# A two-block model on one core: the hybrid layer's elementwise work leaves GpSimd, and block 1's token-major projections run 512 columns per matmul

## The chip, the core and the metric

The kernel runs on one core of a Trainium2 chip. The time is the device time of one execution in microseconds (us); three executions of the kernel before were timed. The engines are written as in the profile: PE (TensorE matmuls), PEld (its weight loads), DVE (VectorE), ACT (ScalarE), POOL (GpSimd) and SP (SyncE, which issues the weight transfers).

## The reference

256 tokens of width 1024 pass through two models one after the other. Block 1 has two layers, each with one large input projection, three branches (differential attention, a gated spatial unit, dilated-window attention) and gated output projections. Block 2 puts 16 meta tokens in front (272 tokens) and has two layers, each of the form feed-forward, mixer, feed-forward. The first mixer is the hybrid one: a forgetting attention ("fox", 8 heads of 64) beside a gated delta rule (4 heads of 128). The second mixer is RWKV-7. Cut to what the change touches:

```python
def layer(x, ...):                                  # block 1, twice
    proj = rmsnorm(x, norm_g) @ w_in                # aq ak av az buv bz cq ck cv cz gates
    ...                                             # attention a, spatial unit b, attention c
    return x + merged @ w_out

def hybrid_attention_mixer(h, w_in, ...):           # block 2, layer 0
    fq, fk, fv, ff, gqkv, ga, gb, gz = split(h @ w_in)
    q, k, v = silu(causal_conv4(gqkv))              # 4 heads of 128
    q, k = l2_normalize(q) / sqrt(128), l2_normalize(k)
    # gated delta rule with decay g and beta, chunked; forgetting attention beside it
    return concat(o_fox, o_gdn) @ w_out
```

## The kernel before

All weights stream from HBM in units of 128x1024 f32 (512 KB). `Stream.unit` (L202 to L213) turns the raw tile `wraw` into a rounded half `wh` by ACT (L210) and the remainder `wl = wraw - wh` (L212), by DVE or, where the stream's rule says so, by POOL. Activations are split in the same way (`xh`, `xl`), and every product is three matmuls: high by high, high by low, low by high. Up to three `wh` and three `wl` tiles exist at a time.

**Block 1.** `proj_tok` (L387) makes the token-major projections: two PSUM banks, one for each 128 tokens, 512 output columns each. Seven such projections are in a layer (cq, ck, cv, aq, ak, av, bv), four units each. A unit holds 4 of the 8 k-tiles for 256 of the 512 columns, so that each matmul writes 256 columns. A `yield` after every three matmuls hands over to `Weave`, which inserts attention steps and delayed pieces (`put_off(n, fn)` runs `fn` after n such steps). The matmuls of these parts carry L96, the line of the helper `Pinned` that fixes their program order; other engines' instructions may be moved by the scheduler.

**The hybrid mixer** (`hybrid`, L985) has 29 units of 24 matmuls. The part called the first stretch below runs units 0 to 12 and then 15, 14, 13: unit 0 gives the small columns, then each head has a k, a q and a v unit. The convolution of each unit is four passes (`cvy`: ACT L1153, then three of DVE, L1155) and a tanh gate (ACT L1157, DVE L1158). Twenty steps later PE turns the result (`ct`), and for q and k `normed` (L1173) takes sums of squares on ACT (L1178), a small power on POOL (`rr`), a halving of it on DVE (L1182) and the scaled copy `kn` on DVE (L1184); twelve steps later PE turns `kn` back (`sm`). `decays` (L1117) makes the decay matrices `iX`, `Ua` and `at`; `gram` (L1203) makes `kqT`, `qd`, and, in `products`, `kd` and `kbe`, all on POOL before. PE runs its instructions in the written order, so that it waits at `sm` for `kn` whatever lies behind. The second stretch begins with `compact16` (L905): the triangular inverse and the delta rule's chunks (`chain`) are interleaved with the fox attention and the units that are left.

Of the kernel before, what the change touches and what calls it, by code (L numbers as in the profile page):

```python
# [371 lines left out]
def block1_layer(c, l, xT, head, pos, ws, w_br, w_out, sgu_w, sgu_b, sgu_gb):  # L372

    nc, tc, ap, tp = c.nc, c.tc, c.b1a, c.b1t
    lam_init = 0.8 - 0.6 * math.exp(-0.3 * l)
    xh, xl, acc = head
# [3 lines left out]
    pe = Pinned(c, nc.tensor)  # L380
    wv = Weave()

    def next_unit():
        unit[0] += 1
        return ws.unit(unit[0] - 1)

    def proj_tok(evac):  # L387

        pss = [bank(c), bank(c)]
        for p in range(2):  # L390
            for kh in range(2):
                wh, wl = next_unit()
                wh4 = wh.rearrange("p (m k c) -> p m k c", m=2, k=4)
                wl4 = wl.rearrange("p (m k c) -> p m k c", m=2, k=4)
                for i in range(2):
                    o = pss[i][:, 256 * p:256 * p + 256].rearrange("p (m c) -> p m c", m=2)
                    for k4 in range(4):
                        k = 4 * kh + k4
                        a, b = xh[:, k, P * i:P * i + P], xl[:, k, P * i:P * i + P]
                        h, w = wh4[:, :, k4, :], wl4[:, :, k4, :]  # L400
                        pe.matmul(o, a, h, start=k == 0, stop=False)
                        pe.matmul(o, a, w, start=False, stop=False)
                        pe.matmul(o, b, h, start=False, stop=k == 7)
                        if p and kh and k4 == 3:
                            evac(i, pss[i])
                        yield

    def rope_T(res, scale):

# [96 lines left out]
    qT, kT, v = qk(), qk(), v2()  # L506
# [135 lines left out]
    vb = [T(c, ap, [P, 512], F32, "vb", bufs=2) for i in range(2)]  # L642
# [27 lines left out]
    pe = nc.tensor  # L670
# [76 lines left out]
    for m in range(KT):  # L747
        wh, wl = wo.unit(m)
# [38 lines left out]
CH = 96  # L787
# [196 lines left out]
def hybrid(c, h, acc, w_in, w_out):  # L984
    nc, tc = c.nc, c.tc  # L985
# [7 lines left out]
    pe, gp = Pinned(c, nc.tensor), Pinned(c, nc.gpsimd)  # L993
    wv = Weave()

    xh, xl = x_pair(c)
    for k in range(KT):
        split(c, xh[:, k, :], xl[:, k, :], h[:, k, :], col(c, "mix0", k))
    ws = Stream(c, w_in, lambda u: u > 3 and (u % 3 == 2 if u < 13 else u % 2 == 0))

    def proj(u, evac):
        wh, wl = ws.unit(u)
# [13 lines left out]
    tri = T(c, cp, [CH, PADT], F32, "tri")  # L1016
# [17 lines left out]
    be, be2 = T(c, ap, [CH, 3, 4], F32, "beta"), T(c, ap, [CH, 3, 4], F32, "beta2")  # L1034
# [5 lines left out]
    gct = T(c, ap, [CH, 3, 4], F32, "gct")  # L1040
    kdf = T(c, ap, [CH, 3, 4], F32, "kdf")
    bgf = T(c, ap, [CH, 3, 4], F32, "bgf")
    U = T(c, ap, [CH, 12, CH], F32, "Ua")
    at = T(c, ap, [CH, 12, CH], F32, "at")
    egc, brc = [t.rearrange("p h (i t) -> p h i t", i=3) for t in (grow, brow)]
# [71 lines left out]
    def decays():  # L1117

        de = T(c, ap, [CH, 12, CH], F32, "iX")
        gp.tensor_sub(de.rearrange("p (h i) t -> p h i t", h=4), egc[:CH],  # L1120
                      gct.rearrange("p i h -> p h i").unsqueeze(3).to_broadcast([CH, 4, 3, CH]))
        nc.vector.tensor_scalar(de, de, 0.0, None, ALU.min)
        keep(nc.scalar.activation(de, de, AF.Exp))

        def masked():
            nc.vector.tensor_mul(U, de, mneg.unsqueeze(1).to_broadcast([CH, 12, CH]))
            gp.tensor_mul(at, de, tri[:, :CH].unsqueeze(1).to_broadcast([CH, 12, CH]))

        wv.put_off(8, masked)
        keep(nc.scalar.activation(egc, egc, AF.Exp))  # L1130
        keep(nc.scalar.activation(kdf, kdf, AF.Exp))
        keep(nc.scalar.activation(bgf, gct, AF.Exp))
        nc.vector.tensor_mul(bgf, bgf, be)


    kd = T(c, ap, [CH, 4, 3, P], F32, "kd")
# [34 lines left out]
    def normed(hd, w):  # L1171


        def then(pt):
            ss = T(c, tp, [CH, 3], F32, "ss", bufs=2)
            for i in range(3):
                sq = T(c, tp, [CH, P], F32, "sqh", bufs=2)
                nc.scalar.activation(sq, pt[:, i, :], AF.Square, accum_out=ss[:, i:i + 1])  # L1178
            nc.vector.tensor_scalar(ss, ss, 0.25, EPS, ALU.mult, ALU.add)
            rr = T(c, tp, [CH, 3], F32, "rr", bufs=2)  # L1180
            gp.tensor_tensor(rr, ss, c.mhalf[:CH, :3], ALU.pow)
            nc.vector.tensor_scalar(rr, rr, 0.5 * P ** -0.5 if w else 0.5, None, ALU.mult)  # L1182
            kn = T(c, tp, [CH, 3, P], F32, f"kn{w}", bufs=2 - w)
            nc.vector.tensor_mul(kn, pt, rr.unsqueeze(2).to_broadcast([CH, 3, P]))  # L1184

            def back():
                pb = bank(c, "sm")
                for i in range(3):
                    pe.transpose(pb[:, CH * i:CH * i + CH], kn[:, i, :], c.ident[:CH, :CH])
                pb3 = pb[:, :PADT].rearrange("p (i t) -> p i t", i=3)  # L1190
                if w == 0:
                    kT = T(c, ap, [P, 3, CH], F32, "kT", bufs=2)
                    nc.scalar.activation(kT, pb3, AF.Copy)
                    KQ[hd] = kT, T(c, ap, [P, 3, 2, CH], F32, "kqT", bufs=2), kn
                else:
                    nc.scalar.activation(KQ[hd][1][:, :, 1, :], pb3, AF.Copy)
                    wv.put_off(12, lambda: gram(hd))

            wv.put_off(12, back)

        return then

    def gram(hd):  # L1203

        kT, kq, kn = KQ[hd]
        gp.tensor_mul(kq[:, :, 0, :], kT, brc[:, hd])
        gp.tensor_mul(qd[:, hd], kq[:, :, 1, :], egc[:, hd])

        def products():
            gp.tensor_mul(kd[:, hd], kn, kdf[:, :, hd:hd + 1].to_broadcast([CH, 3, P]))  # L1210
            gp.tensor_mul(kbe[:, hd], kn, bgf[:, :, hd:hd + 1].to_broadcast([CH, 3, P]))
            for i0, m in ((0, 2), (2, 1)):
                ps = bank(c, "sm")
                for i in range(m):
                    pe.matmul(ps[:CH, 2 * CH * i:2 * CH * (i + 1)], kT[:, i0 + i, :],
                              kq[:, i0 + i].rearrange("p a t -> p (a t)"), start=True, stop=True)
                p4 = ps[:CH, :2 * CH * m].rearrange("p (i a t) -> p i a t", a=2, t=CH)
                for w, o in ((0, U), (1, at)):
                    o = o[:, 3 * hd + i0:3 * hd + i0 + m, :]
                    nc.vector.tensor_mul(o, p4[:, :, w, :], o)  # L1220

        wv.put_off(12 if hd == 0 else 8, products)

    def beta_v(hd):
        def then(pt):
            nc.vector.tensor_mul(vb[:, hd], pt, be2[:, :, hd:hd + 1].to_broadcast([CH, 3, P]))

        return then

# [187 lines left out]
    for hd in range(4):  # L1417
        a = gts[hd]
# [396 lines left out]
def b1_host(I):  # L1815
    a = {}
    a["xT"] = np.ascontiguousarray(I["x"][0].T.reshape(KT, P, TOK1).transpose(1, 0, 2))
    a["pos"] = np.ascontiguousarray(I["positions"].reshape(2, P).T)
    names = ["aq", "ak", "av", "az", "bu", "bv", "bz", "cq", "ck", "cv", "cz", "gA", "gB", "gC"]
    base, n = {}, 0  # L1820
    for nm in names:
        base[nm] = n
        n += 8 if nm[0] == "g" else 4
    order = []
    for nm in ["cq", "ck", "cv", "aq", "ak", "av", "bz", "bu", "bv", "cz", "gC", "gB", "az", "gA"]:
        if nm[1] in "qkv":
            for p in range(2):
                for kh in range(2):
                    order += [(4 * kh + k4, base[nm] + 2 * p + m) for m in range(2) for k4 in range(4)]
        else:  # L1830
            for m in range(8 if nm[0] == "g" else 4):
                order += [(k, base[nm] + m) for k in range(8)]
    br = [(4 * n + k, m) for n in (2, 1, 0) for m in range(8) for k in range(4)]
    sq = [(k, m) for m in range(8) for k in range(8)]
    for l in range(2):

        w = I["w_in"][l]
        qk = w[:, :2 * 512].reshape(D, 2, 2, 2, 2, 64).transpose(0, 1, 2, 4, 3, 5).reshape(D, 1024)
# [125 lines left out]
```

## Time and profile before

| | |
|---|---|
| median of 3 runs | 2030.96 us (2029.15 to 2035.1) |
| the profiled execution's own time | 2033.22 us |
| its span in the profile | 2031.5 us |
| PE, DVE, ACT, POOL busy in the span | 95%, 68%, 48%, 14% |
| the hybrid's first stretch | 838.95 to 923.89 us of the span |
| the hybrid's second stretch | 923.89 to 1039.40 us |

The stretches are read from the trace: the first begins with DVE's first scaled copy of a hybrid projection (L1057), the second with `compact16` and ends where the mixer's output projection begins. Busy shares are means over parts with different limits; what a part is worth is read from that part.

### The profile page before, as it was taken

How to read it: one execution, taken by the hardware profiler on the slowest of the kernel's cores; microseconds unless marked ns; L12 is line 12 of the kernel's file. 1: busy time of each engine (PE TensorE's matmuls, PEld its weight loads, DVE VectorE, ACT ScalarE, POOL GpSimd, SP SyncE). 2: the span in 40 equal slices, each digit the busy share in tenths (PEclk: the TensorE clock that was granted, in tenths of full speed). 3: DMA queues.
4: the chain of work that ended last, by engine and by line, in shares of the span. 5: the costliest groups of instructions: out<-in, count | busy, mean ns of one | idle time of the engine just before them, and what ended most of it. 6: DMA issues, size and time to landing. Idle time of an engine off the chain costs nothing.

```text
span 2031.5 us, 37801 instructions
## 1 busy us (share of the span) xinstructions
PE 1929.5 (95%) x15003; PEld 1858.0 (91%) x15003; DVE 1390.8 (68%) x2896; ACT 973.2 (48%) x1745; POOL 285.1 (14%) x320
## 2 busy tenths in 40 slices
PE   8999999999999999968999999999989879989998
PEld 7889999889999999966999999999988768979998
DVE  6577576577578665787477665666589699846764
ACT  5455355455355444442354444444366535555443
POOL 1113011113010000143010000000044313110000
PEclk9999899999899999987999999999989789989999
DMA  6445466445455555532235555555534100026663
GB/s 200 137 123 160 142 180 181 142 117 161 141 177 176 177 175 174 164 107 63 63 112 169 175 175 176 171 175 174 171 94 135 42 12 1 32 72 180 186 186 115
DMA packets 79461, 280.02 MB, mean 138 GB/s; under 512 B 9890, under 2 KB 12082, under 8 KB 79156
## 3 DMA queue, kind: packets, MB, share of 16 engines
q1 hardware_dynamic: 77088, 275.57, 45.5%
q8 instruction: 118, 1.93, 0.4%
q10 hardware_dynamic: 2196, 2.03, 0.3%
q14 instruction: 59, 0.48, 0.1%
HBM read 276.50 MB, written 1.07 MB: 137 GB/s over the span
## 4 chain that ended last, share of the span: by engine, by line
PE 64%; DVE 9%; ACT 2%; POOL 2%; issue 1%; DVEq 0%; ACTq 0%; POOLq 0%
PE mm L220 17%; PE mm L218 16%; PE mm L219 16%; PE mm L96 4%; PE iv L96 1%; PE iv L946 1%; DVE wl L212 1%; PE fs L96 1%; PE sm L1677 1%; DVE mixt L1523 1%; DVE iYc L925 1%; DVE ish L924 1%; DVE ish L923 0%; PE sm L264 0%; ACT wh L210 0%
## 5 line engine op out<-in xcount | busy, mean ns | idle before, releaser
L210 ACT ACTIVATE wh<-wraw 128x1024 fp32r<-128x1024 f32 x517 | 546.9, 1059 | 603.6 <-PE mm L219 288.8
L212 DVE TENSOR_TENSOR wl<-wraw,wh 128x1024 fp32r<-128x1024 f32 x474 | 587.1, 1239 | 254.9 <-ACT wh L210 249.6
L218 PE MATMUL mm<-xh,wh 128*128 128x272 f32 (+1 forms) x2112 | 607.4, 288 | 5.9 <-ACT xh L1524 3.0
L220 PE MATMUL mm<-xh,wl 128*128 128x272 f32 (+1 forms) x2112 | 606.2, 287 | 6.6 <-DVE wl L212 2.9
L219 PE MATMUL mm<-xl,wh 128*128 128x272 f32 (+1 forms) x2112 | 606.9, 287 | 0.9 <-POOL xl L1526 0.9
L220 PEld LDWEIGHTS mm<-xh,wl 128*128 128x128 f32 x2112 | 401.5, 190 | 9.0 <-DVE wl L212 5.1
L218 PEld LDWEIGHTS mm<-xh,wh 128*128 128x128 f32 x2112 | 399.7, 189 | 7.9 <-ACT xh L1524 3.5
L219 PEld LDWEIGHTS mm<-xl,wh 128*128 128x128 f32 x2112 | 401.1, 190 | 1.9 <-POOL xl L1526 1.3
L218 PE MATMUL mm<-uh,wh 128*128 128x272 f32 (+1 forms) x704 | 201.7, 286 | 0.0
L219 PE MATMUL mm<-ul,wh 128*128 128x272 f32 (+1 forms) x704 | 201.5, 286 | 0.0
L220 PE MATMUL mm<-uh,wl 128*128 128x272 f32 (+1 forms) x704 | 201.0, 286 | 0.0
L212 POOL TENSOR_TENSOR wl<-wraw,wh 128x1024 fp32r<-128x1024 f32 x43 | 103.0, 2396 | 412.4 <-ACT wh L210 368.8
L96 PE MATMUL mm<-wh,xh 128*128 128x256 f32 x448 | 133.9, 299 | 9.2 <-ACT wh L210 9.2
L220 PEld LDWEIGHTS mm<-uh,wl 128*128 128x128 f32 x704 | 133.2, 189 | 0.0
L218 PEld LDWEIGHTS mm<-uh,wh 128*128 128x128 f32 x704 | 132.3, 188 | 0.0
L219 PEld LDWEIGHTS mm<-ul,wh 128*128 128x128 f32 x704 | 132.3, 188 | 0.0
L96 PE MATMUL mm<-wl,xh 128*128 128x256 f32 x448 | 127.4, 284 | 0.7 <-DVE wl L212 0.7
L96 PE MATMUL mm<-wh,xl 128*128 128x256 f32 x448 | 126.6, 283 | 0.0
L96 PE MATMUL mm<-xh,wh 128*128 128x272 f32 (+1 forms) x360 | 120.0, 333 | 0.0
L96 PE MATMUL mm<-xh,wl 128*128 128x272 f32 (+1 forms) x360 | 107.0, 297 | 0.0
L96 PE MATMUL mm<-xl,wh 128*128 128x272 f32 (+1 forms) x360 | 106.8, 297 | 0.0
L96 PEld LDWEIGHTS mm<-wh,xh 128*128 128x128 f32 x448 | 86.1, 192 | 9.2 <-ACT wh L210 9.2
(597 smaller groups left out, 3576.9 us busy)
## 6 DMA issues: line engine op xcount, KB each, us to landing
wraw<-in_ffn_in SPq DMA_DIRECT2D x176, 512.0 KB, 3.6
wraw<-in_w_in SPq DMA_DIRECT2D x136, 512.0 KB, 3.7
wraw<-in_ffn_out SPq DMA_DIRECT2D x88, 512.0 KB, 3.7
wraw<-in_hyb_in SPq DMA_DIRECT2D x29, 512.0 KB, 3.7
wraw<-in_w_br SPq DMA_DIRECT2D x24, 512.0 KB, 3.8
wraw<-in_rw_rkv SPq DMA_DIRECT2D x24, 512.0 KB, 3.8
wraw<-in_w_out SPq DMA_DIRECT2D x16, 512.0 KB, 4.4
wraw<-in_hyb_out SPq DMA_DIRECT2D x8, 512.0 KB, 3.7
```

The source lines that it names most:

```text
L96: return lambda *a, **k: self.tc.keep_in_program_order(f(*a, **k))
L210: nc.scalar.activation(wh, r, AF.Copy)
L212: eng.tensor_sub(wl, r, wh.bitcast(F32))
L218: pe.matmul(ps, lh, rh, start=start, stop=False)
L219: pe.matmul(ps, lh, rl, start=False, stop=False)
L220: pe.matmul(ps, ll, rh, start=False, stop=stop)
L924: nc.vector.tensor_mul(sh, sh, Uc[:, :, j:j + 1].to_broadcast([n, ni, 16 - j]))
L925: nc.vector.tensor_add(Yc[:, :, j:], Yc[:, :, j:], sh)
L946: pe.matmul(ps[:n, n * i:n * i + n], lhs[:, i0 + i, :], rhs[:, i0 + i, :], start=True, stop=True)
L1523: nc.vector.scalar_tensor_tensor(t, xx[:, k, :], col(c, "mu", 8 * i + k), hn[:, k, 1:], ALU.mult, ALU.add)
L1677: nc.tensor.matmul(ps[:, P * q:P * q + P], pair_ht(bd[:, c0 + q]), pair_ht(AR[:, c0 + q]), start=True, stop=True)
```

## The change

In block 1 a unit of a token-major projection now holds 2 of the 8 k-tiles for all 512 columns, and each matmul writes 512 columns; the host packs the weights to match. The number of units, of yields and of columns is as before; the number of matmuls in `proj_tok` halves, from 1344 to 672 over both layers. A step between two yields is now two matmuls and one in turn.

In the hybrid mixer 11 `wl` tiles move from POOL to DVE, as do the decay difference `iX`, the mask of `at`, and the products `kqT` and `qd` (8). `kd` and `kbe` (8 products of 96x384 on POOL) become 24 ACT copies of 96x128 with a factor per token. `kn` (8) and `vb` (4), DVE multiplies before, become 36 ACT copies of the same kind. The halving of `rr` is folded into the constants ahead of the power. POOL keeps the powers and the fills.

```diff
     def proj_tok(evac):
-        for p in range(2):
-            for kh in range(2):
-                wh, wl = next_unit()
...
-                        pe.matmul(o, a, h, start=k == 0, stop=False)
-                        pe.matmul(o, a, w, start=False, stop=False)
-                        pe.matmul(o, b, h, start=False, stop=k == 7)
...
+        for kq in range(4):
+            wh, wl = next_unit()
+            for i in range(2):
+                for k2 in range(2):
...
+                    pe.matmul(pss[i], a, h, start=k == 0, stop=False)
+                    pe.matmul(pss[i], a, w, start=False, stop=False)
+                    yield
+                    pe.matmul(pss[i], b, h, start=False, stop=k == 7)
...
-    ws = Stream(c, w_in, lambda u: u > 3 and (u % 3 == 2 if u < 13 else u % 2 == 0))
+    ws = Stream(c, w_in)
...
-        gp.tensor_sub(de.rearrange("p (h i) t -> p h i t", h=4), egc[:CH],
+        nc.vector.tensor_sub(de.rearrange("p (h i) t -> p h i t", h=4), egc[:CH],
...
-            gp.tensor_mul(at, de, tri[:, :CH].unsqueeze(1).to_broadcast([CH, 12, CH]))
+            nc.vector.tensor_mul(at, de, tri[:, :CH].unsqueeze(1).to_broadcast([CH, 12, CH]))
...
-            nc.vector.tensor_scalar(rr, rr, 0.5 * P ** -0.5 if w else 0.5, None, ALU.mult)
-            nc.vector.tensor_mul(kn, pt, rr.unsqueeze(2).to_broadcast([CH, 3, P]))
+            for i in range(3):
+                nc.scalar.activation(kn[:, i, :], pt[:, i, :], AF.Copy, scale=rr[:, i:i + 1])
...
-        gp.tensor_mul(kq[:, :, 0, :], kT, brc[:, hd])
-        gp.tensor_mul(qd[:, hd], kq[:, :, 1, :], egc[:, hd])
+        nc.vector.tensor_mul(kq[:, :, 0, :], kT, brc[:, hd])
+        nc.vector.tensor_mul(qd[:, hd], kq[:, :, 1, :], egc[:, hd])
...
-            gp.tensor_mul(kd[:, hd], kn, kdf[:, :, hd:hd + 1].to_broadcast([CH, 3, P]))
-            gp.tensor_mul(kbe[:, hd], kn, bgf[:, :, hd:hd + 1].to_broadcast([CH, 3, P]))
+            for i in range(3):
+                nc.scalar.activation(kd[:, hd, i, :], kn[:, i, :], AF.Copy, scale=kdf[:, i, hd:hd + 1])
+                nc.scalar.activation(kbe[:, hd, i, :], kn[:, i, :], AF.Copy, scale=bgf[:, i, hd:hd + 1])
...
-            nc.vector.tensor_mul(vb[:, hd], pt, be2[:, :, hd:hd + 1].to_broadcast([CH, 3, P]))
+            for i in range(3):
+                nc.scalar.activation(vb[:, hd, i, :], pt[:, i, :], AF.Copy, scale=be2[:, i, hd:hd + 1])
```

The scheduler's order on two engines is shown at the place where head 1's k is normed, early in the first stretch. On DVE before, from the clamp of `iX` to the scaled copy `kn` that PE waits for:

```order
L1122 TENSOR_SCALAR iX_10468<-iX_10468 96x1152
L1155 SCALAR_TENSOR_TENSOR cvy_10446<-cvx_10443,cols_80,cvy_10446 128x272
L1179 TENSOR_SCALAR ss_10483<-ss_10483 96x3
L1148 TENSOR_TENSOR cvx_10511<-mm_10461,R_10019 128x272
L1155 SCALAR_TENSOR_TENSOR cvy_10446<-cvx_10443,cols_80,cvy_10446 128x272
L1182 TENSOR_SCALAR rr_10491<-rr_10491 96x3
L212 TENSOR_TENSOR wl_10661<-wraw_10658,wh_10660 128x1024
L1158 SCALAR_TENSOR_TENSOR cvy_10446<-gth_10452,cvy_10446 128x272
L1184 TENSOR_TENSOR kn_1839_10494<-ct_10479,rr_10491 96x384
```

On DVE now, at the same place (lines are three lower; `iX` is no longer made on POOL):

```order
L1117 TENSOR_TENSOR iX_9800<-hgrow_9355,gct_9357 96x1152
L212 TENSOR_TENSOR wl_9859<-wraw_9856,wh_9858 128x1024
L1152 SCALAR_TENSOR_TENSOR cvy_9716<-cvx_9713,cols_80,cvy_9716 128x272
L1119 TENSOR_SCALAR iX_9800<-iX_9800 96x1152
...
L1130 TENSOR_TENSOR bgf_9359<-bgf_9359,beta_9349 96x12
L1123 TENSOR_TENSOR Ua_9360<-iX_9800,mneg_9339 96x1152
L1152 SCALAR_TENSOR_TENSOR cvy_9778<-cvx_9775,cols_80,cvy_9778 128x272
L1178 TENSOR_SCALAR ss_9815<-ss_9815 96x3
L1124 TENSOR_TENSOR at_9361<-iX_9800,tri_9336 96x1152
```

`iX`, `at` and a `wl` have joined DVE's row, `kn` and the halving have left it, and the sums `ss` now stand behind `Ua`.

On ACT before, the same place: the sums of squares of head 1's k, and behind them at once the `wh` of unit 10.

```order
L1178 ACTIVATE sqh_10484,ss_10483<-ct_10479 96x128
L1178 ACTIVATE sqh_10486,ss_10483<-ct_10479 96x128
L1178 ACTIVATE sqh_10488,ss_10483<-ct_10479 96x128
L210 ACTIVATE wh_10660<-wraw_10658 128x1024
L1123 ACTIVATE iX_10468<-iX_10468 96x1152
```

On ACT now, the `wh` of unit 10 is the last row here; the sums of squares of head 1's k stand some twenty instructions ahead of it.

```order
L1183 ACTIVATE kn_1839_9825<-ct_9811,rr_9823 96x128 x3
L1211 ACTIVATE kbe_9363<-kn_1793_9618,bgf_9359 96x128
L1192 ACTIVATE kT_9910<-sm_9906 128x288
L1210 ACTIVATE kd_9362<-kn_1793_9618,kdf_9358 96x128
L1211 ACTIVATE kbe_9363<-kn_1793_9618,bgf_9359 96x128
L1183 ACTIVATE kn_1853_9888<-ct_9874,rr_9886 96x128 x3
L1210 ACTIVATE kd_9362<-kn_1793_9618,kdf_9358 96x128
L1150 ACTIVATE cvy_9919<-cvx_9916,cols_80 128x272
L1154 ACTIVATE gth_9853<-cvy_9847 128x272
L1227 ACTIVATE vb_9364<-ct_9944,beta_1730_9350 96x128 x3
...
L1195 ACTIVATE kqT_9912<-sm_9963 128x3x96
L210 ACTIVATE wh_10000<-wraw_9998 128x1024
```

The copies with a factor per token have moved in ahead of that `wh`, among them two `kn`, each of which waits for a power of POOL.

## Rows read from the trace of the kernel before

**Rows 1.** Windows: from:to, length, PE, PEld, DVE, ACT, POOL busy, PEclk, DMA.

```profile
838.95:923.89 84.94, 65.64 (x461) 61.64 (x460) 71.92 (x139) 39.82 (x109) 40.35 (x54) 0.90 0.39 122
923.89:1039.40 115.51, 108.72 (x840) 97.14 (x840) 69.96 (x205) 39.57 (x110) 19.19 (x23) 0.91 0.19 56
865.00:875.00 10.00, 2.99 (x23) 2.59 (x22) 8.26 (x12) 7.82 (x23) 4.45 (x5) 0.92 0.57 190
875.00:880.00 5.00, 3.52 (x17) 3.52 (x18) 5.00 (x10) 1.47 (x2) 1.75 (x2) 0.50 0.36 108
885.00:890.00 5.00, 4.21 (x22) 4.05 (x23) 4.38 (x13) 2.22 (x4) 0.10 (x1) 0.71 0.30 107
905.00:910.00 5.00, 5.00 (x24) 4.96 (x25) 2.77 (x7) 2.56 (x8) 0.11 (x1) 0.50 0.14 32
930.00:940.00 10.00, 9.80 (x43) 7.52 (x43) 5.49 (x34) 3.34 (x9) 0.11 (x1) 0.58 0.00 0
950.00:965.00 15.00, 13.13 (x59) 10.29 (x59) 8.61 (x32) 4.12 (x13) 2.40 (x2) 0.66 0.18 61
```

**Rows 2.** Timeline, DVE and POOL, 859 to 886 us: start, duration, instruction.

```profile
859.53 0.44 DVE L1148 TENSOR_TENSOR cvx<-mm,R 128x272 f32<-128x272 f32 x1
...
870.14 0.16 DVE L1179 TENSOR_SCALAR ss<-ss 96x3 f32<-96x3 f32 x1
...
871.81 2.61 POOL L96 TENSOR_TENSOR at<-iX,tri 96x1152 f32<-96x1152 f32 x1
...
871.87 3.64 DVE L212 TENSOR_TENSOR wl<-wraw,wh 128x1024 fp32r<-128x1024 f32 x1
...
875.79 0.54 DVE L1184 TENSOR_TENSOR kn<-ct,rr 96x384 f32<-96x384 f32 x1
...
880.85 0.94 POOL L96 TENSOR_TENSOR kd<-kn,kdf 96x384 f32<-96x384 f32 x1
...
881.03 4.15 DVE L1155 SCALAR_TENSOR_TENSOR cvy<-cvx,cols,cvy 128x272 f32<-128x272 f32 x1
...
882.55 2.33 POOL L212 TENSOR_TENSOR wl<-wraw,wh 128x1024 fp32r<-128x1024 f32 x1
```

**Rows 3.** Two DVE lines, 845 to 1045 us: count, shortest/median/longest ns, first and last start.

```profile
L1155 DVE SCALAR_TENSOR_TENSOR cvy<-cvx,cols,cvy x33: 485/495/4147, 848.5 to 912.3; 128x272 f32<-128x272 f32 x33
L212 DVE TENSOR_TENSOR wl<-wraw,wh x16: 1210/1218/3643, 849.4 to 1042.8; 128x1024 fp32r<-128x1024 f32 x16
```

**Rows 4.** Chain that ended last, 840 to 1045 us: start, duration, what.

```profile
876.48 0.71 PE sm L96 x3
...
923.89 4.13 DVE iP L905
```

**Rows 5.** Groups by form, 845 to 1045 us: busy us, mean ns | idle before.

```profile
L1155 DVE SCALAR_TENSOR_TENSOR cvy<-cvx,cols,cvy 128x272 f32<-128x272 f32 x33 | 24.7, 750 | 2.1 <-ACT cvy L1153 2.0
L212 DVE TENSOR_TENSOR wl<-wraw,wh 128x1024 fp32r<-128x1024 f32 x16 | 22.4, 1402 | 2.2 <-ACT wh L210 2.2
...
L96 POOL TENSOR_TENSOR rr<-ss,mhalf 96x3 f32<-96x3 f32 x8 | 8.2, 1021 | 20.9 <-DVE ss L1179 18.1 <-DVE gct L1111 2.8
...
L1178 ACT ACTIVATE sqh<-ct 96x128 f32<-96x128 f32 x24 | 6.1, 259 | 0.2 <-PE ct L96 0.2
...
L1153 ACT ACTIVATE cvy<-cvx,cols 128x272 f32<-128x272 f32 x11 | 5.7, 515 | 6.9 <-PE ct L96 5.3 <-issue 1.6
L1157 ACT ACTIVATE gth<-cvy 128x272 f32<-128x272 f32 x12 | 5.1, 427 | 16.2 <-DVE cvy L1155 16.1
...
L1184 DVE TENSOR_TENSOR kn<-ct,rr 96x384 f32<-96x384 f32 x8 | 4.4, 547 | 0.1
...
L1126 DVE TENSOR_TENSOR Ua<-iX,mneg 96x1152 f32<-96x1152 f32 x1 | 1.3, 1337 | 0.0
```

**Rows 6.** Windows of two feed-forward stretches, 272 and 256 columns per matmul.

```profile
1200.00:1300.00 100.00, 100.00 (x804) 100.00 (x803) 58.55 (x79) 44.34 (x60) 0.85 (x1) 1.00 0.59 173
...
1870.00:1970.00 100.00, 100.00 (x845) 100.00 (x844) 68.73 (x100) 49.71 (x70) 0.00 (x0) 1.00 0.62 185
```

More of the change, by code (lines that the diff above doesn't have):

```diff
@@ L389, in proj_tok @@
         pss = [bank(c), bank(c)]
-        for p in range(2):
-            for kh in range(2):
-                wh, wl = next_unit()
[L393 to L400, printed above, removed]
-                        pe.matmul(o, a, h, start=k == 0, stop=False)
-                        pe.matmul(o, a, w, start=False, stop=False)
-                        pe.matmul(o, b, h, start=False, stop=k == 7)
-                        if p and kh and k4 == 3:
-                            evac(i, pss[i])
-                        yield
+        for kq in range(4):
+            wh, wl = next_unit()
+            for i in range(2):
+                for k2 in range(2):
+                    k = 2 * kq + k2
+                    a, b = xh[:, k, P * i:P * i + P], xl[:, k, P * i:P * i + P]
+                    h, w = wh[:, 512 * k2:512 * k2 + 512], wl[:, 512 * k2:512 * k2 + 512]
+                    pe.matmul(pss[i], a, h, start=k == 0, stop=False)
+                    pe.matmul(pss[i], a, w, start=False, stop=False)
+                    yield
+                    pe.matmul(pss[i], b, h, start=False, stop=k == 7)
+                    if k == 7:
+                        evac(i, pss[i])
+                    yield
     def rope_T(res, scale):
@@ L1119, in decays @@
         de = T(c, ap, [CH, 12, CH], F32, "iX")
-        gp.tensor_sub(de.rearrange("p (h i) t -> p h i t", h=4), egc[:CH],
-                      gct.rearrange("p i h -> p h i").unsqueeze(3).to_broadcast([CH, 4, 3, CH]))
+        nc.vector.tensor_sub(de.rearrange("p (h i) t -> p h i t", h=4), egc[:CH],
+                             gct.rearrange("p i h -> p h i").unsqueeze(3).to_broadcast([CH, 4, 3, CH]))
         nc.vector.tensor_scalar(de, de, 0.0, None, ALU.min)
@@ L1178, in then @@
                 nc.scalar.activation(sq, pt[:, i, :], AF.Square, accum_out=ss[:, i:i + 1])
-            nc.vector.tensor_scalar(ss, ss, 0.25, EPS, ALU.mult, ALU.add)
+            f = 4.0 * P if w else 4.0
+            nc.vector.tensor_scalar(ss, ss, 0.25 * f, EPS * f, ALU.mult, ALU.add)
             rr = T(c, tp, [CH, 3], F32, "rr", bufs=2)
             gp.tensor_tensor(rr, ss, c.mhalf[:CH, :3], ALU.pow)
-            nc.vector.tensor_scalar(rr, rr, 0.5 * P ** -0.5 if w else 0.5, None, ALU.mult)
             kn = T(c, tp, [CH, 3, P], F32, f"kn{w}", bufs=2 - w)
-            nc.vector.tensor_mul(kn, pt, rr.unsqueeze(2).to_broadcast([CH, 3, P]))
+            for i in range(3):
+                nc.scalar.activation(kn[:, i, :], pt[:, i, :], AF.Copy, scale=rr[:, i:i + 1])
             def back():
@@ L1826, in b1_host @@
         if nm[1] in "qkv":
-            for p in range(2):
-                for kh in range(2):
-                    order += [(4 * kh + k4, base[nm] + 2 * p + m) for m in range(2) for k4 in range(4)]
+            order += [(k, base[nm] + m) for k in range(8) for m in range(4)]
         else:
```

## The prediction

> **What bounds the kernel now.** I read the busy time of the engines over the whole span first, then windows of 5 us over the hybrid mixer, then the timeline of DVE and POOL there, and last the chain that ended last. Over the feed-forward stretches PE has no gap at all [rows 6]; nothing of the change lies there. The hybrid mixer is the part that is not full: in its first stretch PE is busy for 65.6 of 84.9 us, while DVE is busy for 71.9 [rows 1]. So 19.3 us are PE's waits. The clock adds to them: after a wait the granted clock is at its lower level, 0.50 and 0.71 in two of the windows and 0.50 in a third, which costs 3.52 x 0.50 + 4.21 x 0.29 + 5.00 x 0.50 = 5.5 us of busy time at half speed [rows 1]. The second stretch has 6.8 us of waits and, at 0.58 and 0.66, 9.80 x 0.42 + 13.13 x 0.34 = 8.6 us of slow clock [rows 1]. The most that the hybrid can give, PE's order being fixed, is 19.3 + 5.5 + 6.8 + 8.6 = 40 us.
>
> Why does PE wait, with DVE busy? The timeline shows it. A convolution pass of DVE, 0.495 us at its median, lasts 4.15 us from 881.03 on, while POOL runs kd, kbe and a wl behind each other until 884.88; a wl of DVE, 1.22 us at its median, lasts 3.64 us while POOL multiplies at [rows 2, 3]. In this trace DVE's two-input work stands still as long as POOL's tensor work runs. Counted over the mixer, the convolution passes lose 33 x (750 - 495) ns = 8.4 us and the wl 16 x (1402 - 1218) ns = 2.9 us [rows 3, 5], and the multiply that opens the second stretch takes 4.13 us where another one of its shape takes 1.34 [rows 4, 5]. The longest wait of PE follows from it: in the 10 us from 865 on it is busy for 2.99 [rows 1], and goes on at 876.48, with the turn of kn [rows 4], which DVE finished late because the wl of 3.64 us stood in front [rows 2].
>
> **Block 1, 512 columns.** 272 columns take 100 us / 804 = 124.4 ns from start to start, 256 columns 100 / 845 = 118.3 ns [rows 6]. At the upper clock level, one column a cycle, 113.3 and 106.7 ns of this are columns; 11.1 and 11.6 ns are not, and I take 11.3 ns for each matmul. proj_tok saves 672 matmuls: 672 x 11.3 ns = 7.6 us. If all of the time went with the columns, it would save nothing. If the two rows are taken as a line, 16 columns cost 6.1 ns, 512 columns 215.9 ns, and a pair saves 236.6 - 215.9 = 20.7 ns, in all 13.9 us. I take 7.6, between the two, because a column cannot cost less than a cycle.
>
> The Trainium skill, "TensorE: Matmul & The Clock Gate", section "Back-to-back issue gap", gives a warm gap of N / 2.4 + 2.5 ns without weight loads, 215.8 ns for 512 columns; for 256 it says 109.2, where this trace has 118.3. By it the term would be 672 x 20.8 ns = 14.0 us.
>
> **The hybrid's first stretch.** DVE gets five wl (1.22 each [rows 3]), iX and at (1.34 each, the shape of Ua [rows 5]) and eight products of 128x288, for which I take the convolution pass of 128x272, 0.5 each [rows 3]: 6.1 + 2.7 + 4.0 = 12.8 us. It loses kn and vb, 12 x 0.547 = 6.6 us [rows 5]. So 6.2 us are added, and the standstills, 11.3 us in the two counted groups, go; DVE's 71.9 us shrink to about 67. ACT gets 60 copies of 96x128. Their price is not in the trace. The square of that shape takes 0.259 us, and a factor per partition adds 515 - 427 = 88 ns at 272 columns [rows 5], so I take 0.35 each, 21 us; between 0.259 each, 15.5 us, and 0.515, the larger shape, 31 us. With 39.8 before [rows 1] ACT comes to 61 us. PE needs 65.6 - 5.5 = 60 us at the upper level. All three fit in 85 us with room; none alone sets the end.
>
> What PE waits for then, worked out at the longest wait. From the copy at 859.53 to the sums ss at 870.14 DVE took 10.6 us; the power, the halving, the wl of 3.64 and kn came after, until 876.33 [rows 2]. Now the row up to ss holds three copies, six convolution passes, two wl, iX, its clamp, kqT, Ua and small ones: 1.3 + 3.0 + 2.4 + 1.3 + 0.7 + 0.5 + 1.3 + 0.9 = 11.4 us, the clamp taken at half of iX. It begins about 0.5 us earlier, since a kn has left DVE ahead of it. So ss is ready near 870.5, the power 1.02 later [rows 5], three copies of ACT 1.05 after that, and PE's turn starts near 872.5 instead of 876.48: 4 us. Of the waits, 19.3 - 7.0 - 1.5 = 10.8 us are left, nearly all behind that point, and with them 3.7 us of slow clock [rows 1]. I take 8 of these 14 us as gained: DVE's standstills there go, but a new wait takes some back. The wh of unit 10 now stands on ACT behind kqT and two kn, and its wl on DVE behind the four products of gram; PE reaches that unit right after gram, so it waits there for about one wl and its queue, 2 to 3 us, and the two kn that wait for powers cost ACT about as much again. In sum 12 us; between 0 and 24.8.
>
> **The hybrid's second stretch.** The opening multiply gives 4.13 - 1.34 = 2.8 us [rows 4, 5], and PE's chain goes through it. A shorter wait there may keep the clock from falling: the slow 10 us behind it cost 4.1 us [rows 1], and I take half, 2 us. Six wl move to DVE here, 7.3 us, which has 115.5 - 70.0 = 45 us free [rows 1]; POOL's held DVE as well, so I count them at nothing. If each of them stood in front of the attention's chain, they would cost 7.3. In sum 5 us; between 15.4 gained and 7.3 lost.
>
> **The sum.** 7.6 + 12 + 5 = 24.6 us from the profiled execution's 2033.2: 2008.6. That execution lies 2.3 us above the median of the three runs, so I forecast 2007 us for a median.
>
> **Rivals.** First, **more**: with DVE free, PE hardly waits and its clock stays up. Two thirds of the hybrid's 40 us and 14 of block 1 give 41, so 1990 us. For it speaks that all three engines have room; against it, that kn now passes DVE, POOL and ACT in turn.
>
> Second, **ACT takes DVE's place**. Each of the eight kn waits in ACT's queue for ss and the power, and the next wh stands behind it. POOL waited 20.9 / 8 = 2.6 us for ss and took 1.02 [rows 5]; were ACT to stand still for both each time, its 61 us would be 61 + 8 x 3.6 = 90, and the stretch 5 us longer than now. With 7.6 and 5 gained elsewhere that leaves 2033.2 - 7.6 - 5 + 5 - 2.3 = 2023 us. Against it: between two kn the scheduler has put other work in ACT's row. About 2023 is also what comes out if the standstills of DVE have another cause than POOL, so that only block 1 gains.
>
> Third, **slower**: the same queue, at a higher price. For a loss of 6 us the first stretch has to grow by 6 + 7.6 + 5 = 18.6 us, to 103.5; ACT's waits then are 103.5 - 61 = 42.5 us, 5.3 us for each kn. At 6 us each the time is 2033.2 - 7.6 - 5 + 24 - 2.3 = 2042 us. It decides only if the late wh of each head stops PE, so that the next sums are late too.
>
> The Trainium skill, "ScalarE: Activation LUTs", section "Rules for kernel authors", says to put multiplies on VectorE and not on ScalarE, which speaks against this part. Here the rows bear it out by price, 0.547 us on DVE against about 1.05 us in three copies on ACT; it would turn the sum only by the second or third rival.
>
> **How the numbers follow.** The forecast gets 0.58, with a range of its own from 1997 to 2016; more 0.14; ACT in DVE's place, or only block 1, 0.20; slower 0.05; the rest, 0.03, is no change. 0.3%, about 6 us, is what a measurement of this kernel can tell from no change. A quarter of the second rival falls inside that, so: faster 0.58 + 0.14 + 0.15 = 0.87, same 0.03 + 0.05 = 0.08, slower 0.05. The range that holds 8 of 10 reaches from 1991, into the first rival, to 2024, over the second.
>
> **What will show it.** Right: in the hybrid's first stretch no convolution pass over 1 us, DVE busy near 60 to 67 us and ACT near 60, the stretch shorter by about 12 us; the opening multiply of the second stretch near 1.34 us; the 512-column matmuls about 225 ns apart. Wrong: long DVE instructions while POOL does only powers; ACT idle in front of kn for 3 us or more at each head; 512 columns 236 ns or more apart; PE's waits in the second stretch grown at the moved wl.

## The result and the profile after

The changed kernel takes 2006.66 us (median of 4 runs, 2001.78 to 2008.37) where the kernel before takes 2032.26 (4 runs, 2029.15 to 2035.1): a ratio of 0.986, 95% interval 0.983 to 0.989. The forecast was 2007. The sum came out right, but two of its terms did not, in opposite directions.

I cut the profiled execution (span 2005.2 us, before 2031.5) at the places where it was cut before: the first convolution input of the hybrid (`cvx` of 32 rows), the opening multiply of the second stretch (`iP` from `Ua`), and the start of the hybrid's output projection. These are windows of the changed kernel, columns as in [rows 1]:

```profile
835.86:908.53 72.67, 61.36 (x461) 57.51 (x460) 56.58 (x133) 55.37 (x169) 11.20 (x31) 0.98 0.43 136
908.53:1011.73 103.20, 100.40 (x839) 90.11 (x838) 69.43 (x210) 39.26 (x109) 4.53 (x16) 1.00 0.21 67
```

Beside [rows 1]: the way to the hybrid is 838.95 - 835.86 = 3.1 us shorter, the first stretch 84.94 - 72.67 = 12.3, the second 115.51 - 103.20 = 12.3. What follows is longer by 1.4.

The single instructions (count, shortest/median/longest ns, first and last start):

```profile
L1152 DVE SCALAR_TENSOR_TENSOR cvy<-cvx,cols,cvy x36: 484/495/503, 839.2 to 896.3; 128x272 f32<-128x272 f32 x36
L902 DVE TENSOR_TENSOR iP<-Ua,bm x1: 1346/1346/1346, 908.5 to 908.5; 96x1152 f32<-96x1152 f32 x1
L1183 ACT ACTIVATE kn<-ct,rr x24: 352/358/366, 849.8 to 901.3; 96x128 f32<-96x128 f32 x24
L1210 ACT ACTIVATE kd<-kn,kdf x12: 391/398/404, 862.8 to 902.1; 96x128 f32<-96x128 f32 x12
```

No convolution pass is over 0.51 us, where one took 4.15 [rows 3]; the opening multiply takes 1.35 us where it took 4.13 [rows 4]. A copy of ACT lasts 0.36 to 0.40 us.

TensorE's four largest waits over both stretches, first before the change, then after it (line, what it waited for, us in total, times, longest):

```profile
PE sm L96 <- DVE kn L1184: 11.4, 2, 7.6
PE ft L96 <- ACT fs L1277: 3.5, 1, 3.5
PE sm L96 <- DVE at L1220: 3.4, 1, 3.4
PE fs L96 <- DVE fqT L1260: 2.1, 2, 1.9
```

```profile
PE sm L96 <- DVE at L1220: 4.3, 2, 3.3
PE sm L96 <- ACT kn L1183: 3.3, 1, 3.3
PE mm L96 <- DVE wl L212: 1.9, 1, 1.9
PE ft L96 <- ACT fs L1278: 1.2, 2, 0.8
```

The wait for kn shrinks from 11.4 to 3.3 us. The wait of 1.9 us for a wl is new: it is the one forecast at unit 10. The wait for gram's products (`at`) stays. And five 512-column matmuls, from the timeline of block 1 (start, duration):

```profile
64.46 0.39 PE L96 MATMUL mm<-wl,xh 128*128 128x512 f32 x1
64.69 0.39 PE L96 MATMUL mm<-wh,xl 128*128 128x512 f32 x1
64.92 0.40 PE L96 MATMUL mm<-wh,xh 128*128 128x512 f32 x1
65.16 0.40 PE L96 MATMUL mm<-wl,xh 128*128 128x512 f32 x1
65.39 0.39 PE L96 MATMUL mm<-wh,xl 128*128 128x512 f32 x1
```

They start 0.23 to 0.24 us apart; over the four steps from 64.46 to 65.39 it is 0.93 / 4 = 232 ns.

### The profile page after: what moved, and what is told of

Same layout as the page of the kernel before. It is cut to its first block, busy times and chain, and to the rows that moved or that the text cites. A ratio compares the mean times of both kernels' runs of the same rounds, so it can differ in the third digit from the quotient of the medians.

```text
span 2005.2 us, 36481 instructions
## 1 busy us (share of the span) xinstructions
PE 1914.5 (95%) x14331; PEld 1808.6 (90%) x14331; DVE 1373.3 (68%) x2897; ACT 990.0 (49%) x1805; POOL 246.8 (12%) x291
## 4 chain that ended last, share of the span: by engine, by line
PE 82%; DVE 10%; ACT 3%; POOL 3%; issue 1%; DMA 0%; DVEq 0%; POOLq 0%; ACTq 0%
PE mm L220 19%; PE mm L218 19%; PE mm L219 19%; PE mm L96 12%; PE sm L96 2%; DVE wl L212 1%; PE iv L96 1%; PE iv L943 1%; PE po L96 1%; PE fs L96 1%; ACT wh L210 1%; DVE mixt L1524 1%; PE sm L1678 1%; DVE iYc L922 1%; PE sm L264 0%
## 5 line engine op out<-in xcount | busy, mean ns | idle before, releaser
L212 DVE TENSOR_TENSOR wl<-wraw,wh 128x1024 fp32r<-128x1024 f32 x485 | 596.9, 1231 | 255.9 <-ACT wh L210 250.7
L212 POOL TENSOR_TENSOR wl<-wraw,wh 128x1024 fp32r<-128x1024 f32 x32 | 81.4, 2544 | 339.8 <-ACT wh L210 306.5
L96 PE MATMUL mm<-wh,xh 128*128 128x512 f32 x224 | 95.2, 425 | 9.0 <-ACT wh L210 9.0
L96 PE MATMUL mm<-xl,wh 128*128 128x272 f32 (+1 forms) x360 | 103.2, 287 | 0.0
L219 PE MATMUL mm<-yl,wh 128*128 128x256 f32 x320 | 91.2, 286 | 0.5 <-DVE yl L228 0.5
L220 PE MATMUL mm<-yh,wl 128*128 128x256 f32 x320 | 90.6, 284 | 0.0
L96 PE MATMUL mm<-wh,xl 128*128 128x512 f32 x224 | 90.5, 404 | 0.0
```

Of the source, the lines that this page charges most:

```text
L96: return lambda *a, **k: self.tc.keep_in_program_order(f(*a, **k))
L212: eng.tensor_sub(wl, r, wh.bitcast(F32))
L219: pe.matmul(ps, lh, rl, start=False, stop=False)
L220: pe.matmul(ps, ll, rh, start=False, stop=stop)
```

## The experiments

My theory after the result: VectorE and GpSimd keep each other from working; taking GpSimd's tensor work out frees VectorE, TensorE's waits get shorter, and in the second stretch the clock no longer falls. The rival: the chains got shorter because no product is fetched from GpSimd any more. All ratios are against the kernel before, timed on the same chip.

**1 to 4: the parts alone.** e1 has only proj_tok and its packing, e2 only `ws = Stream(c, w_in)`, e3 only the products, e4 the whole hybrid part with 256-column matmuls in block 1.

> The kernel before with the 512-column matmuls of block 1 alone. First theory: a pair of 256-column matmuls takes 2 x 118.3 = 236.6 ns, one of 512 columns in the changed kernel 232 ns (starts at 64.92, 65.16 and 65.39), so 672 x 4.6 ns = 3.1 us less, all of it before the hybrid layer, ratio 0.9985; the hybrid's two stretches stay at 84.9 and 115.5 us. Rival: block 1 gives the 7.6 us of the prediction and something else in it took back 4.5; then a stretch of block 1 without 512-column matmuls is longer here than before.

> The kernel before with the eleven wl of the hybrid on VectorE and all its products left on GpSimd. First theory (VectorE stands still while GpSimd does two-input work): 11 x 2.4 = 26 us of such work go, but the opening multiply of the second stretch still stands behind kd and kbe (4.1 us) and the clock still falls after it; 3 us shorter in each stretch, 2026 us in all. Rival (the products' hops through GpSimd cost, the wl cost nothing): no change in the first stretch, and in the second nothing or a loss up to 7 us, since VectorE now has 7.3 us more of its own to do.

> The kernel before with all products of the hybrid moved as in the change (iX, at, kqT and qd to VectorE, kd, kbe, kn and vb to ACT), the eleven wl left on GpSimd. First theory: the opening multiply of the second stretch takes 1.35 us where it took 4.13, the clock stays at its upper level behind it, and the second stretch loses some 9 of the 12.3 us that the whole change takes from it; the first stretch loses about 8 of 12.3, since five wl of GpSimd still hold VectorE; in all 2015 us. Rival (the hops): all of 12.3 in both stretches, 2009 us.

> The whole change of the hybrid layer with block 1 as before. First theory: parts add up, 2032.3 - 25.6 + 3.1 = 2009.8 us, ratio 0.989; stretches of the hybrid at 72.6 and 103.2 us as in the changed kernel. Rival: the shorter block 1 shifts the hybrid's loads and so took part in its gain; then the two stretches are over 2 us longer than that.

Measured: e1 0.998 (0.995 to 1.000), e2 0.992 (0.990 to 0.994), e3 0.998 (0.995 to 1.000), e4 0.990 (0.988 to 0.992). The two stretches of e2, e3 and e4, in this order:

```profile
838.37:912.68 74.31, 62.24 (x461) 58.31 (x460) 66.17 (x143) 40.43 (x109) 30.88 (x49) 0.95 0.43 139
912.68:1024.41 111.73, 109.13 (x839) 97.55 (x838) 70.20 (x210) 39.33 (x109) 5.12 (x17) 0.91 0.18 57
```

```profile
837.87:911.96 74.09, 63.70 (x461) 59.81 (x460) 58.99 (x128) 55.24 (x169) 23.68 (x37) 0.93 0.39 133
911.96:1033.70 121.74, 117.92 (x839) 104.66 (x839) 67.79 (x204) 39.52 (x109) 17.84 (x22) 0.83 0.18 57
```

```profile
838.60:911.64 73.04, 62.66 (x461) 58.87 (x460) 56.65 (x133) 55.18 (x169) 11.21 (x31) 0.95 0.42 135
911.64:1014.85 103.21, 100.41 (x838) 90.12 (x837) 69.44 (x210) 39.24 (x109) 4.51 (x16) 1.00 0.20 67
```

Block 1 behaves as expected: e1 reaches the hybrid at 834.6 us, the kernels with 256 columns (before, e2, e3, e4) at 837.9 to 838.95; the eight profiles with 512 columns and no other change in block 1 lie between 833.1 and 835.9, on the mean 3.6 us earlier. Its whole time says no more than that something is gained. The hybrid's parts don't add up, against both my expectations. In the first stretch either one alone gives about 10.7 us and both give 12: once VectorE is relieved by either, the waits that are left are others. In the second stretch the wl alone give 3.8 us, the products alone lose 6.2, and both give 12.3; each is one execution, and e1, whose second stretch is that of the kernel before, took 120.6 us there against 115.5, so that much of e3's loss can be the spread of the clock. The rival in its plain form falls with e2: there all products are still fetched from GpSimd, and it has 18.5 of the 23.1 us that e4 gains (TensorE's waits before hold none for a wl, so that a wl that comes sooner does not explain it). But the products no longer stand behind a wl in GpSimd's row there; e5, below, is the cleaner test. What differs in the second stretch is less the waits (PE idle 2.6, 3.8 and 2.8 us) than TensorE's busy time at 109.1, 117.9 and 100.4 us for the same matmuls, with the clock at 0.91, 0.83 and 1.00. In e3 the opening multiply still takes 2.75 us, with a wl of GpSimd beside it, and the clock stands near 0.50 from 917 to 937 us.

**5 and 6: work on GpSimd that nobody reads.** In the changed kernel, behind each of the eleven wl and where the products stood:

```
+            nc.gpsimd.tensor_sub(ws.last, wh.bitcast(F32), wh.bitcast(F32))
+        gp.tensor_mul(scr[:p, :n], x[:p, :n], x[:p, :n])
```

Here `ws.last` is the raw tile of the unit that has just been split, and `scr` is scratch. In e6 these are `tensor_copy` with one input.

> The changed kernel, with two-input work put back on GpSimd at the places where it stood before, written into scratch that nobody reads (a subtraction of 128x1024 behind each of the eleven wl, squares of 96x256 and 128x256 where iX, at, kqT, qd, kd and kbe stood); the work of the layer itself stays where the change put it. First theory (VectorE stands still as long as GpSimd's two-input work runs): convolution passes of 2 us and more come back, VectorE's busy time in the first stretch rises from 56.6 to 68 us or more, the first stretch from 72.7 to 80 us or more, and the whole to 2020 us or more. Rival (the gain came from shorter chains, since no result is fetched from GpSimd any more): nobody waits for this work, so 2007 us and passes of 0.5 us.

> The same as the run before it, but the work put back on GpSimd has one input (copies, of half as many elements more behind each wl, so that GpSimd is busy about as long). If any tensor work of GpSimd holds VectorE: the same as the run before it, 2020 us or more. If only its two-input work does: convolution passes stay at 0.5 us and the whole at 2007 us within 3 us.

Measured: e5 0.994 (0.992 to 0.996), e6 0.992 (0.989 to 0.994). First e5, then e6, the first stretch:

```profile
835.46:919.10 83.64, 66.29 (x462) 61.77 (x460) 67.61 (x133) 55.70 (x169) 41.31 (x65) 0.92 0.34 111
```

```profile
835.58:916.45 80.87, 64.76 (x461) 60.63 (x460) 62.46 (x133) 55.64 (x169) 39.22 (x72) 0.92 0.36 115
```

Two groups of VectorE, first e5, then e6, and the copies of GpSimd in e6:

```profile
L1165 DVE SCALAR_TENSOR_TENSOR cvy<-cvx,cols,cvy x36: 482/501/2253, 838.8 to 906.9; 128x272 f32<-128x272 f32 x36
L1166 DVE SCALAR_TENSOR_TENSOR cvy<-cvx,cols,cvy x36: 479/494/1543, 838.9 to 905.1; 128x272 f32<-128x272 f32 x36
L96 POOL COPY scr<-tri x8: 398/634/2977, 860.8 to 869.4; 96x256 f32<-96x256 f32 x8
```

VectorE has the same 133 instructions as in the changed kernel, and they take 67.6 and 62.5 us instead of 56.6. e5 gives back 11 of the 12.3 us of the first stretch although no result of this work is used. So it is GpSimd's being at work that costs, and it suffices. The longest convolution pass is 2.25 us in e5 and 1.54 in e6. That only two-input work of GpSimd holds VectorE is refuted by e6, whose whole time lies between what I expected of the two cases. It works the other way round too: a copy of 96x256 on GpSimd takes 0.40 to 2.98 us in e6, and in the changed kernel a power of three numbers took 2.24 us instead of 1.02 because a multiply of VectorE had begun just before it:

```profile
864.71 1.35 DVE L1124 TENSOR_TENSOR at<-iX,tri 96x1152 f32<-96x1152 f32 x1
...
864.88 2.24 POOL L96 TENSOR_TENSOR rr<-ss,mhalf 96x3 f32<-96x3 f32 x1 [5.28 <-DVE ss L1178]
```

The Trainium skill, "SBUF — State Buffer", section "Who interferes with whom", tells of a pair of ports that VectorE and GpSimd share: whichever issues first has it for a whole instruction, and the other stands still. These two rows agree with it, and so does e6.

Two other ways for this work to cost time are to be looked at. GpSimd's powers stand behind it in GpSimd's row, and it writes into the raw tiles, so that the next load into such a tile starts later. ACT's waits for GpSimd in front of kn in the first stretch (the profile names the power or the small fill beside it), in the changed kernel, e5 and e6, two rows each:

```profile
ACT kn L1183 <- POOL cvx L96: 5.7, 4, 2.0
ACT kn L1183 <- POOL rr L96: 2.3, 2, 1.5
ACT kn L1196 <- POOL cvx L96: 5.1, 3, 2.1
ACT kn L1196 <- POOL rr L96: 3.1, 3, 1.3
ACT kn L1197 <- POOL rr L96: 6.2, 4, 3.2
ACT kn L1197 <- POOL cvx L96: 3.6, 2, 2.3
```

And TensorE's three largest waits in the first stretch of e5:

```profile
PE sm L96 <- DVE at L1238: 6.7, 2, 5.7
PE ct L96 <- DVE cvy L1168: 3.3, 2, 2.7
PE sm L96 <- ACT kn L1196: 2.6, 1, 2.6
```

ACT waits 8.0, 8.2 and 9.8 us for GpSimd. In e5 TensorE waits no longer for kn than in the changed kernel (2.6 us, there 3.3); what grew are its waits for VectorE, at from 4.3 to 6.7 and cvy from nothing to 3.3. The late powers are thus no part that shows in e5; in e6 the wait for kn grew to 5.3 us, and they may have a share that these runs don't separate. The later loads reach nobody: TensorE's wait for a wl is 2.4 and 1.9 us (1.9 in the changed kernel), and ACT shows no wait for a load. Of the 11 us of e5, 6.0 are TensorE's idle time and 4.9 the same matmuls at a lower clock (0.92 instead of 0.98).

**7 and 9: is it the length of TensorE's wait that lets the clock fall?** e7 repeats the opening multiply, e9 puts a scan in front of it:

```
+    for _ in range(3 if n == 96 else 1):          # e7
         nc.vector.tensor_mul(t, U, ...)

+    if n == 96:                                   # e9
+        nc.vector.tensor_tensor_scan(t, U, U, 0.0, ALU.mult, ALU.add)
     nc.vector.tensor_mul(t, U, ...)
```

> The changed kernel with the multiply that opens the hybrid's second stretch carried out three times over (same result), so that it ends 2.7 us later, as late as before the change. First theory (a longer wait of TensorE there lets its granted clock fall, and the fall costs more than the wait): the clock is at 0.50 for some 10 to 20 us behind it, the second stretch is 8 to 13 us longer than 103.2, and the whole 2015 to 2020 us. Rival (the clock was kept up by something else): the stretch is 2.7 us longer, 2009.5 us.

> The changed kernel with one more VectorE instruction, a scan of 96x1152 into the same tile, ahead of the multiply that opens the hybrid's second stretch (its values are overwritten, the result stays). The run with the multiply three times over did not test what it should, since the softmax step that TensorE waits for slipped in between the copies; here it stands behind one instruction of about 3 us instead of one of 1.35. First theory (a longer wait of TensorE there lets its granted clock fall): TensorE waits 1.5 us more, the clock is at 0.50 behind it for 5 us or more, and the second stretch takes 107 us or more (103.2 in the changed kernel), the whole 2011 us or more. Rival (the clock does not hang on that wait): the stretch takes 103 to 105 us, with the clock at 1.00, the whole 2008 us.

e7 measured 0.986 (0.984 to 0.988), as the changed kernel, second stretch 103.6 us: the softmax steps of VectorE (L1278) stood between the copies, at 908.07 and 909.52, so no single hold was longer than 1.35 us. It tells nothing about the clock. e9 measured 0.991 (0.989 to 0.994); its second stretch with four windows from it, its VectorE there, and TensorE's longest wait:

```profile
907.60:1020.52 112.92, 108.55 (x838) 97.22 (x837) 72.31 (x211) 39.08 (x109) 4.51 (x16) 0.91 0.20 61
912.60:917.60 5.00, 3.58 (x15) 2.80 (x15) 3.46 (x12) 0.55 (x2) 0.00 (x0) 0.53 0.17 18
917.60:922.60 5.00, 5.00 (x21) 3.90 (x21) 3.31 (x14) 1.68 (x4) 0.11 (x1) 0.50 0.31 98
922.60:927.60 5.00, 5.00 (x21) 3.72 (x20) 1.52 (x9) 0.82 (x3) 0.15 (x2) 0.50 0.27 97
927.60:932.60 5.00, 5.00 (x28) 4.96 (x27) 3.03 (x18) 1.68 (x3) 0.00 (x0) 0.50 0.00 0
```

```profile
907.60 2.55 DVE L903 TENSOR_TENSOR_SCAN iP<-Ua 96x1152 f32<-96x1152 f32 x1
910.07 0.23 DVE L1279 CUSTOM_DVE_ANT_0 fs<-fs,hrep 96x96 f32<-96x96 f32 x1
```

```profile
PE ft L96 <- ACT fs L1280: 2.0, 1, 2.0
```

The softmax step comes 1.2 us later, and TensorE's longest wait for it is 2.0 us instead of 0.8. The stretch is 9.7 us longer: 1.6 us of it idle, 8.1 us the same matmuls at the lower clock level (0.50 to 0.53 in four windows of 5 us, from 912.6 to 932.6). So a short wait at this place can cost several times its length. The other profiles fit: where TensorE's longest wait there is 1.2 us or more (e2 1.2, e6 1.5, e3 2.2, before and e1 3.5), the clock stands at 0.50 behind it; where it is 0.8 to 1.0 (the changed kernel, e4, e5, e7, e10, e11, e12), it stays at its upper level there. It does not decide alone: in e8, below, the wait was 0.8 us, the multiply took 1.34 us, and the clock fell all the same.

**8: does it matter that ACT applies the factors?** kn, vb, kd and kbe are one VectorE product each; the edit of kn, those of the others are alike:

```
-            for i in range(3):
-                nc.scalar.activation(kn[:, i, :], pt[:, i, :], AF.Copy, scale=rr[:, i:i + 1])
+            nc.vector.tensor_mul(kn, pt, rr.unsqueeze(2).to_broadcast([CH, 3, P]))
```

> The changed kernel with kn, vb, kd and kbe as one VectorE product each in place of three ACT copies each. VectorE gets 20 products of about 0.55 us, 11 us, in the first stretch (56.6 to 67.5 us busy), ACT loses 60 copies of 0.36 to 0.40 us, 22 us (55.4 to 33 us). First theory (both engines have room once GpSimd is silent; where the factors are applied matters little): first stretch 72.7 us within 2, whole 2007 us within 3. Rival (ACT is what made the gain, since kn no longer stands behind a wl on VectorE): first stretch 77 us or more, and with the clock 2013 us or more. Second rival (ACT's copies cost, three instructions for one): 2003 us or less.

Measured: 0.986 (0.984 to 0.988), 2007.16 us, no different from the changed kernel.

```profile
834.66:909.48 74.82, 63.77 (x461) 60.26 (x460) 65.06 (x154) 40.24 (x109) 11.44 (x31) 0.91 0.41 132
909.48:1016.92 107.44, 104.84 (x839) 93.68 (x837) 69.36 (x210) 39.37 (x109) 4.51 (x16) 0.95 0.20 64
```

In this one execution the stretches are 2.2 and 4.2 us longer, all of it TensorE's busy time at a lower clock (its idle time is 11.1 and 2.6 us, in the changed kernel 11.3 and 2.8). The part behind the hybrid, with the same code, took 988.6 us in it, 4.9 less than in the changed kernel's, and the whole times are the same. With GpSimd silent, VectorE has room for these products; ACT's part is not what made the gain.

**10 to 12: more of GpSimd's work moved.** e10 moves block 1's 32 wl, e11 the subtractions of `mix` in the recurrent layer, e12 both:

```
-        ws = [Stream(c, a[f"w_in{l}"], lambda u: u > 3 and u % 4 == 3) for l in range(2)]
+        ws = [Stream(c, a[f"w_in{l}"]) for l in range(2)]

-                    (nc.gpsimd if k > 1 else nc.vector).tensor_sub(xx[:, k, :], ...)
+                    nc.vector.tensor_sub(xx[:, k, :], ...)
-                eng = nc.gpsimd if k % 2 else nc.vector
-                eng.tensor_sub(xl[:, k, :], t, ...)
+                nc.vector.tensor_sub(xl[:, k, :], t, ...)
```

> The changed kernel with the 32 wl that block 1 still has on GpSimd moved to VectorE too. Theory that the hold costs only where VectorE is near its limit: VectorE is busy for 395 of the first 597 us there and TensorE waits 16.6 us, 9 of them for the first weights, so 0 to 3 us are to be had, 2004 to 2007 us. Rival (the hold costs wherever it falls, 32 x 1.2 us of VectorE's time or more): 2000 us or less. Rival on the other side (VectorE's 39 us more stand in the way of softmax steps): 2010 us or more.

> The changed kernel with the 36 subtractions of 128x272 that mix of the second recurrent layer still has on GpSimd (xx, and the odd xl and xml) moved to VectorE: GpSimd loses about 36 us between 1440 and 1530 us, VectorE gets 30 x 0.42 = 13 us more to do where it is near 90% busy. If the hold works here as in the hybrid, VectorE's passes of 0.9 to 1.0 us for mixt go back to 0.43 and the net is a gain of 3 to 8 us, 1999 to 2004 us. Rival (VectorE is the bound here and only gets longer): 2010 us or more.

> The changed kernel with both further moves off GpSimd: the 32 wl of block 1 and the subtractions of mix. In the profiles the first made the way to the hybrid shorter (835.9 to 830.1 us), the second the part behind the hybrid (993.5 to 986.2 us), though neither whole time was told apart from the changed kernel. If both shares are real they add up: hybrid reached at 830 us, 987 us behind it, stretches 73 and 103 us, the whole 1993 to 1998 us, ratio 0.981. Rival (the two shares were the spread of the clock from one execution to the next): 2004 us or more, ratio 0.985.

Measured: e10 0.985 (0.982 to 0.989), e11 0.986 (0.983 to 0.990), e12 0.982 (0.979 to 0.985), 1996.7 us, the fastest median of all. The intervals of e12 and of the changed kernel still overlap a little, so that a gain of the whole is not shown. In the profiles e12 has the two shares: the hybrid is reached at 829.7 us, and the part behind it, in the changed kernel and in e12, is

```profile
1011.73:2005.20 993.47, 933.75 (x7220) 908.11 (x7218) 686.68 (x1503) 485.05 (x859) 117.00 (x156) 0.96 0.42 129
1005.49:1990.50 985.01, 928.64 (x7220) 905.35 (x7218) 684.83 (x1533) 483.40 (x859) 83.53 (x126) 0.96 0.41 131
```

The difference of 8.5 us is too large a figure for the second share: without the move this part takes between 988.6 us (e8) and 995.4 (e1) in twelve profiles, 991.6 on the mean. Both profiles with it lie below that, 986.2 in e11 and 985.0. Nor did it come as I expected: the passes for mixt were 0.49 us at the median before the move and 0.50 after it. The results that GpSimd made in 0.76 to 5.04 us come from VectorE in 0.43 to 1.02; whether this is what gains, no run tests. The way through block 1 up to the same matmul, in the changed kernel, then in e10:

```profile
0.00:597.00 597.00, 580.38 (x3897) 514.65 (x3898) 394.61 (x777) 291.61 (x498) 110.75 (x75) 0.98 0.51 156
```

```profile
0.00:591.20 591.20, 576.08 (x3898) 512.76 (x3899) 406.59 (x809) 292.10 (x498) 29.91 (x43) 0.99 0.51 158
```

VectorE takes over 32 wl (777 instructions become 809) of 1.22 us, 39 us, and is busy for only 406.59 - 394.61 = 12 us more. The other 27 us it had spent standing still before, although it was far from its limit there; so the hold costs VectorE's time wherever it falls. What this is worth to the kernel is less sure. The hybrid is reached at 830.1 us, 5.8 us earlier than in the changed kernel's profile and 3.0 earlier than in the earliest of the eight profiles named above, where I had expected 0 to 3; of the 5.8 us 1.5 are TensorE's idle time and 4.3 its busy time.

## Why the prediction was right, and where it was not

**The sum: right by luck in part.** It forecast 24.6 us for the profiled execution and 26.3 were gained. Block 1 gave 4.5 us less than its term and the second stretch 7.3 more; 1.4 were lost behind the hybrid, where nothing was changed.

**What bounds the hybrid: right.** VectorE stood still while GpSimd worked, and that kept TensorE waiting: put back without a reader, such work lengthened VectorE's instructions and TensorE's waits for them (e5).

**Block 1, 7.6 us: mis-sized.** It gave 3.1. The step that failed is that every matmul costs the same 11.3 ns beside its columns. At 512 columns it is 232 - 213.3 = 18.7 ns, so a pair saves 236.6 - 232 = 4.6 ns and 672 pairs 3.1 us; the profiles reach the hybrid 3.1 to 3.6 us earlier. The figure of the Trainium skill, 215.8 ns in "TensorE: Matmul & The Clock Gate", section "Back-to-back issue gap", lies farther off than mine, 225.

**First hybrid stretch, 12 us: 12.3, by other shares.** The turn of head 1's kn comes at 867.57 us, 31.7 into the stretch where it came at 37.5 [rows 4]: 5.8 us, forecast 4, so that the rest gave 6.5, forecast 8. VectorE came to 56.6 us, not 67: I had counted the standstills of two groups (11.3 us), but with 6.2 us added and 71.9 before, all of them must have been 71.9 + 6.2 - 56.6 = 21.5, or about 20, as the eight halvings of rr that left VectorE too (0.17 us each) were not in my sum. ACT came to 55.4 us (61): a copy lasts 0.36 to 0.40 us (0.35), but its busy time grew by only 15.6 us for 60 of them, 0.26 each, since they overlap (three in a row take 0.85 to 0.88 us). The new wait at unit 10 is there, at 1.9 us (2 to 3).

**Second stretch, 5 us: mis-sized.** It gave 12.3: 4.0 us of waits (6.8 to 2.8; forecast 2.8) and 8.3 us of busy time (108.7 to 100.4; I took 2 for the clock). The clock did not fall once. That I halved the clock's price behind the opening multiply (4.1 us) and left that from 950 us on (4.5) at nothing was the wrong choice; e9 shows that a wait 1.2 us longer can bring 9.7 of the 12.3 us back. The 12.3 us are also those of an execution without a fall: in e8's, with the same multiply, it would have been 8.1.

**The rivals.** "More" had the right mechanism for this stretch. "ACT takes DVE's place" did not happen: ACT stood for 5.7 + 2.3 = 8.0 us in front of all eight kn, 1.0 each, not 3.6. "Only block 1 gains" is refuted by e4, and "slower" by the result; but e3's second stretch, 6.2 us longer than before in one execution, suggests that a part of this change alone can lose by the clock.

**What stays open:** why the clock fell in e8 and not in the changed kernel, with the same multiply; and what of a whole time is due to chance of this kind. The hybrid's second stretch has the same code in e1 as before and took 120.6 us in one execution, 115.5 in the other.

## What to carry over

Work given to GpSimd was not free for VectorE here, near its limit or far from it: the price is read from the longest instruction of a VectorE group beside its median, and from what stands on GpSimd at that moment. In a stretch in which TensorE has short waits, read busy time and granted clock next to the idle time: removing the last wait before a fall can be worth several times that wait. Since one execution's clock can make several microseconds in a part, a part is to be compared over several profiles. Parts of such a change are to be tried together, since each may look small or even harmful alone.

## What the runs showed of the hardware

- One-input copies of GpSimd hold VectorE too (e6: the same 133 instructions take 62.5 us, not 56.6), and VectorE's two-input work holds GpSimd: 0.40 us became 2.98 (e6), 1.02 became 2.24 (changed kernel). VectorE's clamp of `iX`, with one input, is held as well: 2.50 us in e5 beside a subtraction of GpSimd, 0.75 in the changed kernel.
- With 512 columns, matmuls with a weight load each start 232 ns apart, 18.7 ns more than the 213.3 ns of their columns at the upper clock level; with 256 columns it is 11.6 ns more [rows 6].
- Where the clock does not fall, the second stretch takes 103.2 us in every profile that has it so (changed kernel, e4, e10, e11, e12), within 0.05 us; TensorE's longest wait behind the opening multiply is 0.8 us in each of them.
